# A projection tile loaded one unit earlier, and empty steps ahead of its matmuls, in a two-layer decoder trunk

## The chip, the cores and the metric

The kernel runs on one core of a Trainium2 chip. The metric is the device time of one execution in microseconds; the kernel before took 2547.33 us in the median of three runs (2542.2 to 2547.57). The engines are named as in the profile: PE (TensorE, matmuls; PEld are its weight loads), DVE (VectorE), ACT (ScalarE), POOL (GpSimd) and SP (SyncE, which issues most transfers).

## The reference

A residual stream `x` of 1024 tokens by 1024 passes two layers. Layer 0 mixes with native sparse attention (compressed, selected and windowed branches, 16 heads in 4 groups), layer 1 with a sliding window of 128 and a sink per head. Each mixer ends with an output projection, `o.reshape(B, S, 1024) @ w_out`, then `x = x + (1 + g1) * rms_norm(y, norm_g)`, and a squared-ReLU MLP with hidden size 4096 follows:

```python
y = nsa_mixer(h, ...)            # layer 0;  swa_sink_mixer in layer 1
x = x + (1 + g1)[:, None, :] * rms_norm(y, norm_g[i, 1])
h = modulate(rms_norm(x, norm_g[i, 2]), sh2, sc2)
y = squared_relu_mlp(h, mlp_w_up[i], mlp_w_down[i])
x = x + (1 + g2)[:, None, :] * rms_norm(y, norm_g[i, 3])
```

## The kernel before

**Precision.** A product of float32 matrices is made of three matmuls (`mm3`, L572 to L574): each operand is split in a rounded high part and a low part (the rest), and high x high, low x high and high x low are added up in PSUM.

**Attention.** Both attentions are software pipelines of 32 units (`pipeline`, L940). In layer 0 a unit is a token tile `i` of 128 queries and a head group `j`, in the order j = 0 with i = 0 to 7, then j = 1 and so on, so units 24 to 31 are j = 3. In layer 1 the four groups of one token tile follow each other. A unit has *head* steps (scores on the PE, masking with a running minimum on DVE, L884, exponentials on ACT, L888, scaling on POOL, L1028 or L1626) and *main* steps: a turn (`pv_steps`, L890) transposes four probability blocks on the PE (L903) and splits them into a high part (ACT, L909) and a low part (DVE, L910), and three turns later the products with V follow (L925). The head steps of later units are let out at a rate: the summed cost of all heads over the summed weight of all main entries. Between a unit's turns, `spread` deals out the entries that `more(n)` gives for the unit.

**The end of a unit.** In layer 0 the output of a unit is copied (ACT, L1121) and stored to the DRAM tile `od[i]` by SP (L1122). In layer 1 it stays on the chip: `o_out` copies it (ACT, L934 and L936) and adds both halves on POOL (L938) into `o32[i]`.

**Output projection.** `out_steps(t, ...)` returns `first` and eight matmul steps. `first` gets the tile by `load`, casts it to its high part (L1179, DVE), subtracts for the low part (L1180, DVE) and loads the rows of x (L1183, SP). In layer 0 `load` brings the tile from DRAM in four transfers on SP (L1737) and adds two halves on DVE (L1738). A matmul step is two terms of `mm3`, six matmuls; 48 make a tile of 128 x 1024. Behind them the tile is squared (ACT, L513), multiplied by the gate row (DVE, L514), added to x (L522), stored (L1196), normalised and turned for the MLP.

The projection weights (eight `load` steps, each a 512 KB transfer at L547, a cast on ACT at L565 and a subtraction at L566, on POOL in layer 0 and on DVE in layer 1) come in during attention: in layer 0 as entries of units 26 to 31, in layer 1 two each in units 4 to 7.

**Order.** In layer 0 all projection work follows attention: `outs[0][0]` (the `first` of tile 0) stands after the last unit, then each tile's steps with the next tile's `first` ahead of them. In layer 1 the projection is dealt into later units: after unit 6, 10, 14 and so on, `out(i)` appends `first`, NO empty steps and the eight matmul steps to `extra`, of which the following four units take a share each; the last tile stands behind the last unit. Empty steps count as entries, for the rate and for chains that wait some number of steps (`later`, `TURN`). All large buffers come from one pool of 40. The order of instructions on each engine is laid out in the build by the scheduler of `TileContext` (`schedule_with_timeline_sim=True`), from the program's order and the dependences.

Of the kernel before, what the change touches and what calls it, by code (L numbers as in the profile page):

```python
# [45 lines left out]
W0 = 4  # L46
ON = 2
WP = 1
NO = 1
ML = 0  # L50
RAMP1 = 12
HOLD = 80
# [41 lines left out]
class Trunk:  # L94
# [1549 lines left out]
    def run(self):  # L1644
        nc, a = self.nc, self.a
        tok = lambda t: slice(t * P, (t + 1) * P)
        self.cols, self.gates = {}, {}
        self.mark("setup")
        self.setup()
        xin, xout = a["x"][0], self.out[0]  # L1650
        self.mark("start")
        xr = {}
        def load_x(ts):
            xs = [self.slot(name="x") for t in ts]
            for t, x in zip(ts, xs):
                nc.sync.dma_start(x, xin[tok(t)])
            return xs

        def norm_x(ts, xs):
            for stages in zip(*(self.norm_stages(x, xr, t) for t, x in zip(ts, xs))):  # L1660
                for f in stages:
                    f()

        half = self.ada_first()
        (load0, half0), (load1, half1) = half(0), half(1)
        xs = load_x(range(4))
        rows = self.load_columns()
        w_in = a["nsa_w_in"][0]
        raws = []
        for f in load0:  # L1670
            f()
        for k in (0, 2):
            raws.insert(0, self.raw_weight(self.slot, w_in, [k, k + 1], D, 512))
        self.setup_columns(*rows)
        norm_x(range(4), xs)
        hT = [[], []]
        parts = self.nsa_project(hT, w_in)
        loads, steps = parts[0]
        pre = self.pre_pairs([xr[t] for t in range(4)], self.cols[0, 0], hT[0])
        first = lambda k: [steps[4 * t + k + z] for z in range(2) for t in range(4)]  # L1680
        for k in range(PA):
            pre[k][0]()
        for f in half0:
            f()
        for f in load1:
            f()
        for k in (4, 6):
            raws.insert(0, self.raw_weight(self.slot, w_in, [k, k + 1], D, 512))
        self.raws = raws
        for f in loads[:2]:  # L1690
            f()
        xs = load_x(range(4, NT))
        pre = [g if k < PA else lambda f=f, g=g: (f(), g()) for k, (f, g) in enumerate(pre)]
        self.mark("nsaproj")
        second = half1[:-1] + loads[2:] + half1[-1:]
        self.later(self.turn_tables, 6)
        self.go(pre[:4] + spread(second[:-1], first(0)) + second[-1:])
        norm_x(range(4, NT), xs)
        self.setup_late()
        self.go(pre[4:6] + spread(pre[6:], first(2)[:4]))  # L1700
        for f in self.pre_steps([xr[t] for t in range(4, NT)], self.cols[0, 0], hT[1]):
            self.later(f, 0)
        self.go(first(2)[4:])
        side = self.ada_gate(0, 0) + self.ada_pre(0, 1)
        self.chunks([([], steps[16:])] + parts[1:-1] + [(parts[-1][0], parts[-1][1][:QN])], side, [], S0)
        self.flush()

        src = [xin[tok(t)] for t in range(NT)]
        for l in range(2):
            w_out = a["nsa_w_out" if l == 0 else "swa_w_out"][0]  # L1710
            self.mark("att")
            x1 = [self.tc.dram_tile([P, D], F32, name=f"x1_{l}_{t}") for t in range(NT)]
            xr = {}
            o32 = {}
            grow = {}

            def gate(l=l, grow=grow):
                if not grow:
                    grow[0] = self.gate_row(self.gates[l, 0])
                return grow[0]  # L1720

            take, up = self.up_setup(a["mlp_w_up"][l], lambda l=l: self.cols[l, 1])

            def done(t, x, take=take, xr=xr, l=l):
                def turn():
                    self.chain([lambda: None] * (2 + DL if t == NT - 1 else TURN[l]) + take(t, xr))
                self.chain(self.norm_stages(x, xr, t) + [turn])

            if l == 0:
                loads = self.out_weights(w_out, nc.gpsimd if WP & (l + 1) else None)  # L1730

                def load(t):
                    o = [self.slot("o32", F32, [P, KT, P]) for _ in range(2)]
                    for h in range(2):
                        src = self.od[t][64 * h:64 * h + 64].rearrange("d j (k z) t -> z d (j k) t", z=2)
                        for z in range(2):
                            nc.sync.dma_start(o[h][64 * z:64 * z + 64], src[z])  # L1737
                    nc.vector.tensor_tensor(o[0], o[0], o[1], op=ALU.add)  # L1738
                    return o[0]

                def more(n):
                    return {26: loads[0:1], 27: loads[1:2], 28: loads[2:3], 29: loads[3:5], 30: loads[5:6], 31: loads[6:]}.get(n, [])

                self.nsa_attention(more, parts[-1][1][QN:])
                outs = [self.out_steps(t, lambda t=t: load(t), src[t], gate, x1[t], done) for t in range(NT)]
                self.mark("wout")
                outs[0][0]()
                for t in range(NT):
                    steps = outs[t][1]
                    if t + 1 < NT:  # L1750
                        steps = [outs[t + 1][0]] + steps
                    else:
                        steps = spread(up[-1], steps)
                    self.go(steps)
            else:
                extra, loads = list(parts[-1][1][4 * QT:]), self.out_weights(w_out, nc.gpsimd if WP & (l + 1) else None)

                def out(i):
                    f, steps = self.out_steps(i, lambda: o32.pop(i), src[i], gate, x1[i], done)
                    extra.extend([f] + [lambda: None] * NO + steps)  # L1760

                def more(n):
                    k = -(-len(extra) // ((ON - n) % 4 + 1)) if n > ON else len(extra) // (4 + ON - n)
                    part = extra[:k]
                    del extra[:k]
                    if n >= W0:
                        part = spread(loads[:2], part)
                        del loads[:2]
                    if n % 4 == ON and n > ON:
                        out(n // 4 - 1)  # L1770
                    return part

                self.pipeline([self.swa_unit(i, gg, o32) for i in range(NT) for gg in range(4)], more, LEAD2, RAMP, 0, RS2, LAG2)
                out(NT - 1)
                self.go(spread(up[-1], extra))
            self.mark("mlp")
            xd = [self.tc.dram_tile([P, D], F32, name=f"x2_{t}") for t in range(NT)] if l == 0 else \
                [xout[tok(t)] for t in range(NT)]
            hT2 = [[], []]
            xr2 = {}  # L1780
            g2 = []

            def post(t, y, l=l):
                if not g2:
                    g2.append(self.gate_row(self.gates[l, 1]))
                x = self.slot(name="x")
                nc.sync.dma_start(x, x1[t])
                half, stages = self.gated(lambda h: y[:, h * 512:(h + 1) * 512], lambda: x, lambda: g2[0],
                                          nc.gpsimd if t < (PT if l else PT0) else nc.vector)

                def end():
                    nc.sync.dma_start(xd[t], x)
                    if l == 0:
                        self.finish_tile(t, x, xr2, self.cols[1, 0], hT2)
                half(0)
                half(1)
                self.later(lambda: self.chain(stages + [end]), 1)

            if l == 0:
                parts = self.swa_project(hT2, a["swa_w_in"][0])  # L1800
            side = self.ada_gate(0, 1, True) + self.ada_pre(1, 0, None, True) if l == 0 else self.ada_gate(1, 1, True)
            self.mlp(up, a["mlp_w_down"][l], side, self.ada_gate(1, 0) + self.ada_pre(1, 1) if l == 0 else [], post,
                     parts[0][0] if l == 0 else [])
            if l == 0:
                self.mark("swaproj")
                self.chunks(parts[:-1] + [(parts[-1][0], parts[-1][1][:4 * QT])])
                src = xd
            self.flush()
# [28 lines left out]
```

## Time and profile before

| | |
|---|---|
| median of three runs | 2547.33 us |
| profiled execution | 2548.21 us |
| its span in the profile | 2546.4 us |
| mean granted clock of the PE | 0.977 |
| attention of layer 0, ends with the last L925 | at about 789.8 us |
| projection of layer 0 | 796.17 to about 896 us |
| attention and projection of layer 1 | about 1665 to 1903 us |

Times in a timeline are microseconds from the start of the span. A number in brackets at the end of a line is the idle time of that engine just before it, and after the arrow stands what ended it. Consecutive instructions of one kind are merged in one line, with their count.

### The profile page before, as it was taken

To read this page: it belongs to the slowest core of one execution; us is meant where nothing else is said; L and a number is where in the kernel's file an instruction comes from. 1 tells how busy PE (TensorE), PEld (TensorE's weight loads), DVE (VectorE), ACT (ScalarE), POOL (GpSimd) and SP (SyncE) were. 2 spreads that over 40 slices of the span, in tenths; PEclk is the share of its full clock that TensorE was granted. 3 is DMA by queue.
4 is the path that set the end of the run, shared out by engine and by line. 5 is a ranking of instruction groups with operands and counts; after the bars stand their busy time and mean duration, and the time that the engine had idled before them with its cause. 6 is when DMAs were issued, how large, how long until landed. Compare 5 with 4: busy or idle time off the path is not lost.

```text
span 2546.4 us, 36695 instructions
## 1 busy us (share of the span) xinstructions
PE 2399.9 (94%) x11974; PEld 1991.6 (78%) x11974; DVE 1924.9 (76%) x3723; ACT 1403.2 (55%) x2959; POOL 1325.5 (52%) x1308
## 2 busy tenths in 40 slices
PE   6989999999998988999999999978999899999997
PEld 4779788888887766777778887867877688888886
DVE  7866479999895477877899768667767766787756
ACT  4632268888983463444435445367876355545433
POOL 4320566564672146555764722577744654594533
PEclk8999999999999999999999999998999999999999
DMA  7367723131226635556888754444323545597654
GB/s 279 100 224 229 237 88 96 39 92 42 84 71 149 141 116 189 201 191 201 321 324 324 236 189 163 138 128 125 75 76 128 186 168 183 192 318 240 230 183 173
DMA packets 239288, 437.15 MB, mean 172 GB/s; under 512 B 19236, under 2 KB 122872, under 8 KB 239096
## 3 DMA queue, kind: packets, MB, share of 16 engines
q1 hardware_dynamic: 210296, 405.44, 47.3%
q0 software_dynamic: 28800, 29.36, 4.8%
q8 instruction: 94, 1.54, 0.2%
q14 instruction: 98, 0.80, 0.1%
HBM read 320.42 MB, written 114.31 MB: 171 GB/s over the span
## 4 chain that ended last, share of the span: by engine, by line
PE 40%; DVE 6%; POOL 3%; issue 2%; DMA 2%; ACT 2%; SPq 0%; POOLq 0%; DVEq 0%; ACTq 0%
PE b L574 13%; PE b L572 13%; PE b L573 12%; POOL sx L1415 1%; DVE ada L323 1%; PE b L880 1%; DMA w<-in_mlp_w_up_dram 1%; DVE hl L1251 1%; PE o L925 1%; DVE p L884 1%; PE b L903 1%; DVE wt L1340 1%; DMA adaw<-in_ada_w_dram 0%; POOL qv L637 0%; POOL wr L1473 0%
## 5 line engine op out<-in xcount | busy, mean ns | idle before, releaser
L572 PE MATMUL b<-hh,wt 128*128 128x512 f32 x896 | 355.0, 396 | 17.0 <-ACT wt L1339 16.9
L574 PE MATMUL b<-hh,wt 128*128 128x512 f32 x896 | 350.9, 395 | 11.9 <-DVE wt L1340 11.6
L573 PE MATMUL b<-st,st 128*128 128x512 f32 x896 | 350.3, 391 | 4.9 <-DVE st L1489 4.9
L573 PE MATMUL b<-hl,wt 128*128 128x512 f32 x896 | 352.1, 393 | 0.0
L574 PE MATMUL b<-st,st 128*128 128x512 f32 x896 | 349.0, 390 | 0.0
L572 PE MATMUL b<-st,st 128*128 128x512 f32 x896 | 330.7, 390 | 1.6 <-DVE u L1370 1.6
L888 ACT ACTIVATE p<-p,nm 128x256 f32<-128x256 f32 (+7 forms) x384 | 250.7, 657 | 56.5 <-DVE nm L884 55.3
L1028 POOL TENSOR_SCALAR p<-p,rl,nsam 128x640 f32<-128x640 f32 (+7 forms) x256 | 199.5, 791 | 139.5 <-DVE rl L1026 93.1
L910 DVE TENSOR_TENSOR pT<-b,pT 128x512 fp32r<-128x512 f32 (+1 forms) x334 | 215.0, 657 | 19.5 <-ACT pT L909 19.1
L1488 ACT ACTIVATE st<-wr 128x1024 fp32r<-128x1024 f32 (+1 forms) x128 | 122.6, 958 | 193.2 <-POOL wr L1474 87.4
L1489 DVE TENSOR_TENSOR st<-wr,st 128x1024 fp32r<-128x1024 f32 (+1 forms) x128 | 188.3, 1471 | 53.6 <-ACT st L1488 30.1
L1489 DVE TENSOR_TENSOR st<-sr,st 128x1024 fp32r<-128x1024 f32 (+1 forms) x128 | 200.4, 1566 | 33.0 <-ACT st L1488 30.8
L572 PEld LDWEIGHTS b<-hh,wt 128*128 128x128 f32 x896 | 170.1, 190 | 59.3 <-ACT wt L1339 25.4
L574 PEld LDWEIGHTS b<-hh,wt 128*128 128x128 f32 x896 | 169.9, 190 | 55.7 <-DVE wt L1340 20.5
L909 ACT ACTIVATE pT<-b 128x512 fp32r<-128x512 f32 (+1 forms) x334 | 186.3, 579 | 43.2 <-PE b L903 41.8
L573 PEld LDWEIGHTS b<-st,st 128*128 128x128 f32 x896 | 168.5, 188 | 42.4 <-DVE st L1489 7.8
L903 PE MATMUL b<-ident,p 128*128 128x128 f32 x1296 | 193.5, 273 | 5.7 <-DVE nm L884 4.1
L1340 DVE TENSOR_TENSOR wt<-ws,wt 128x512 fp32r<-128x512 f32 x128 | 139.5, 1101 | 77.4 <-ACT wt L1339 76.8
L572 PEld LDWEIGHTS b<-st,st 128*128 128x128 f32 x896 | 168.6, 188 | 37.2 <-DVE u L1370 2.4
L573 PEld LDWEIGHTS b<-hl,wt 128*128 128x128 f32 x896 | 170.1, 190 | 34.6
L574 PEld LDWEIGHTS b<-st,st 128*128 128x128 f32 x896 | 168.6, 188 | 34.9
L925 PE MATMUL o<-pT,kv 128*128 128x512 f32 x484 | 193.1, 437 | 1.8 <-DVE pT L910 1.4
(277 smaller groups left out, 6060.3 us busy)
## 6 DMA issues: line engine op xcount, KB each, us to landing
adaw<-in_ada_w_dram SPq DMA_DIRECT2D x96, 512.0 KB, 4.9
sr<-s SPq DMA_DIRECT2D x96, 512.0 KB, 4.7
wr<-in_mlp_w_down_dram SPq DMA_DIRECT2D x96, 512.0 KB, 5.9
w<-in_mlp_w_up_dram SPq DMA_DIRECT2D x76, 512.0 KB, 4.8
s<-sx SPq DMA_DIRECT2D x64, 512.0 KB, 4.0
x<-x SPq DMA_DIRECT2D x48, 512.0 KB, 3.8
s<-u SPq DMA_DIRECT2D x64, 256.0 KB, 2.3
we<-in_mlp_w_down_dram SPq DMA_DIRECT2D x64, 256.0 KB, 3.9
```

The source lines that it names most:

```text
L572: mm(out, s[0], m[0], start=first, stop=False)
L573: mm(out, s[0], m[1], start=False, stop=False)
L574: mm(out, s[1], m[0], start=False, stop=last)
L888: self.nc.scalar.activation(p, p, AF.Exp, scale=-1.0, bias=nm, accum_out=l)
L903: nc.tensor.transpose(pt[:, g * P:(g + 1) * P], p[:, cols], self.ident)
L909: nc.scalar.activation(x[:, 0, 0:w], pt[:, 0:w], AF.Copy)
L910: nc.vector.tensor_tensor(x[:, 1, 0:w], pt[:, 0:w], x[:, 0, 0:w].bitcast(F32), op=ALU.subtract)
L925: nc.tensor.matmul(out, s, m[:, z], start=n == 0 and z == 0, stop=n == len(tiles) - 1 and z == 1)
L1028: nc.gpsimd.tensor_scalar(ps[g], ps[g], rl[:, g:g + 1], gate[:, g, b:b + 1], op0=ALU.mult, op1=ALU.mult)
L1340: nc.vector.tensor_tensor(lo, r, hi.bitcast(F32), op=ALU.subtract)
L1488: nc.scalar.activation(hi, r, AF.Copy)
L1489: nc.vector.tensor_tensor(lo, r, hi.bitcast(F32), op=ALU.subtract)
```

## The change

The constant NO goes from 1 to 4. In layer 0, the list of `outs` is built ahead of attention, and the `first` of tile 0 becomes an entry of unit 31, between its two weight steps.

```diff
-NO = 1
+NO = 4
...
                 def more(n):
-                    return {26: loads[0:1], 27: loads[1:2], 28: loads[2:3], 29: loads[3:5], 30: loads[5:6], 31: loads[6:]}.get(n, [])
-
+                    return {26: loads[0:1], 27: loads[1:2], 28: loads[2:3], 29: loads[3:5], 30: loads[5:6],
+                            31: loads[6:7] + [outs[0][0]] + loads[7:]}.get(n, [])
+
+                outs = [self.out_steps(t, lambda t=t: load(t), src[t], gate, x1[t], done) for t in range(NT)]
                 self.nsa_attention(more, parts[-1][1][QN:])
-                outs = [self.out_steps(t, lambda t=t: load(t), src[t], gate, x1[t], done) for t in range(NT)]
                 self.mark("wout")
-                outs[0][0]()
                 for t in range(NT):
```

## Rows read from the trace of the kernel before

**Rows 1.** The page, part 1: busy time, share of the span, instructions.

```profile
PE 2399.9 (94%) x11974; PEld 1991.6 (78%) x11974; DVE 1924.9 (76%) x3723; ACT 1403.2 (55%) x2959; POOL 1325.5 (52%) x1308
```

**Rows 2.** Timeline of the PE at the seam of layer 0: start, length, line.

```profile
785.37 1.26 PE L925 MATMUL o<-pT,kv 128*128 128x512 f32 x4
786.86 2.89 PE L925 MATMUL o<-pT,kv 128*128 128x512 f32 x9 [0.22 <-DVE pT L910]
796.17 0.77 PE L572 MATMUL b<-wh,oh 128*128 128x512 f32 x1 [6.43 <-DVE oh L1179]
...
799.73 0.42 PE L572 MATMUL b<-wh,oh 128*128 128x512 f32 x1
799.99 0.39 PE L573 MATMUL b<-wl,oh 128*128 128x512 f32 x1
800.22 0.40 PE L574 MATMUL b<-wh,ol 128*128 128x512 f32 x1
```

**Rows 3.** Windows: length, busy of PE, PEld, DVE, ACT, POOL, clock, DMA, GB/s.

```profile
794.00:798.00 4.00, 1.83 (x4) 1.49 (x5) 3.15 (x3) 0.00 (x0) 0.00 (x0) 0.50 1.14 280
```

**Rows 4.** Timeline of SP, 760 to 790: transfers as they are issued.

```profile
765.05 0.37 SPq L547 DMA_DIRECT2D w<-in_mlp_w_up_dram  x1
779.21 0.34 SPq L1122 DMA_DIRECT2D o<-otmp  x1
782.84 0.37 SPq L547 DMA_DIRECT2D w<-in_mlp_w_up_dram  x1
783.31 2.86 SPq L1737 DMA_DIRECT2D o<-o  x4
```

**Rows 5.** Timeline of DVE, 775 to 806.

```profile
777.76 2.91 DVE L910 TENSOR_TENSOR pT<-b,pT 128x512 fp32r<-128x512 f32 x5 [1.23 <-ACT pT L909]
783.70 1.89 DVE L910 TENSOR_TENSOR pT<-b,pT 128x512 fp32r<-128x512 f32 x3 [3.04 <-ACT pT L909]
786.11 3.08 DVE L910 TENSOR_TENSOR pT<-b,pT 128x512 fp32r<-128x512 f32 x5 [0.52 <-ACT pT L909]
794.00 1.23 DVE L1738 TENSOR_TENSOR o<-o,o 128x1024 f32<-128x1024 f32 x1 [4.81 <-DMA o<-o]
795.33 0.69 DVE L1179 CAST oh<-o 128x1024 fp32r<-128x1024 f32 x1
796.06 1.23 DVE L1180 TENSOR_TENSOR ol<-o,oh 128x1024 fp32r<-128x1024 f32 x1
...
804.69 0.69 DVE L1179 CAST oh<-o 128x1024 fp32r<-128x1024 f32 x1
```

**Rows 6.** L1737's landings; waits of L1738; L1737's issues from 780 to 796.

```profile
DMA to landing us min/median/max: 4.2/6.6/10.1
...
  DMA o<-o: 32.1, 7
...
o<-o SPq DMA_DIRECT2D x8, 256.0 KB, 8.1
```

**Rows 7.** Timelines of ACT and DVE, 840 to 852.

```profile
844.15 0.20 ACT L513 ACTIVATION_READ_ACCUMULATOR junk<-b 128x1 f32 x1
...
849.06 1.22 DVE L1738 TENSOR_TENSOR o<-o,o 128x1024 f32<-128x1024 f32 x1 [7.15 <-DMA o<-o]
850.20 0.68 DVE L514 TENSOR_TENSOR yg<-b,gbc 128x512 f32<-128x512 f32 x1
```

**Rows 8.** Timeline of the PE in layer 1, 1720 to 1730.

```profile
1722.93 0.80 PE L572 MATMUL b<-wh,oh 128*128 128x512 f32 x1 [3.86 <-DVE oh L1179]
1726.37 0.79 PE L574 MATMUL b<-wh,ol 128*128 128x512 f32 x1 [2.22 <-DVE ol L1180]
```

**Rows 9.** Windows in layer 1, columns as in rows 3.

```profile
1715.00:1720.00 5.00, 2.97 (x8) 1.83 (x8) 5.00 (x13) 4.44 (x12) 5.00 (x7) 0.50 0.70 239
1720.00:1725.00 5.00, 1.22 (x2) 0.50 (x2) 5.00 (x14) 4.94 (x16) 4.98 (x7) 0.50 0.86 236
1725.00:1730.00 5.00, 3.63 (x9) 2.85 (x10) 3.90 (x6) 0.56 (x2) 4.79 (x5) 0.50 1.09 260
```

**Rows 10.** Waits of the PE, 1730 to 1910: total us, times, longest.

```profile
PE b L572 <- DVE oh L1179: 2.5, 1, 2.5
PE b L880 <- DVE nm L884: 1.6, 2, 1.3
```

## The prediction

> **What bounds the kernel now.** I read the busy shares first. The PE works 94% of the span, and no other engine gets past 76% [rows 1]. So a microsecond is gained where the PE stands still or runs at the half clock, and hardly anywhere else. I then went to the two seams that the diff touches, with the timelines of PE, DVE and SP side by side, and with the windows for the clock.
>
> At the seam of layer 0, the last attention matmuls end at 789.75, and the first projection matmul starts at 796.17 after 6.43 us of idle, released by the cast of L1179 [rows 2]. The clock falls meanwhile (0.50, that is 1.2 GHz, from 794 to 798 [rows 3]), and the first eight projection matmuls need 3.56 us, where a later one starts 0.23 us after the one before [rows 2]: 3.56 - 8 x 0.23 = 1.7 us lost. The reader should see why the cast is late. SP issues the four loads of L1737 from 783.31 to 786.17, behind a weight load at 782.84, though it did nothing between 765.42 and 779.21 [rows 4]. Then the add of L1738 waits 4.81 us for them until 794.00, and add, cast and subtraction end at 797.29, 3.3 us later [rows 5].
>
> In layer 1, the first projection tile stops the PE for 3.86 us (its cast) and again for 2.22 us (its low half) [rows 8]. Around it DVE, ACT and POOL are all but full and the clock is at 0.50 [rows 9]. The last tile waits another 2.5 us [rows 10].
>
> **Part 1: the first tile goes into unit 31.** Its step issues four loads and the load of x on SP, and add, cast and subtraction on DVE. Three entries spread over 17 steps stand at steps 0, 6 and 12 (two stood at 0 and 9). So the tile comes after the sixth turn, whose DVE copy ends at 780.67 [rows 5], and the last weight step moves from 9 to 12. That weight is needed only late in tile 0, so I cost its move at nothing.
>
> What it costs on DVE: the 3.3 us now stand ahead of eight copies of L910 (three from 783.70, five from 786.11, 4.97 us together). DVE has a hole of 3.04 us there [rows 5]. If the loads have landed by 780.67, the copies slip by 0.3 us. If not, DVE waits at the add, and the copies wait behind it. That an instruction behind it does wait is seen later in this stage: the multiplication of L514 had its input at 844.35, but ran at 850.20, after the add had waited 7.15 us and run [rows 7].
>
> So the term hangs on the landing. The loads take 4.2 us at least, 6.6 in the median, and 8.1 for those issued at this seam [rows 6]. Three cases, each with 13 attention matmuls [rows 2] and 48 projection matmuls to follow (61 x 0.23 = 14.0 us), against tile 0's end today at 799.73 + 40 x 0.23 = 808.9:
> - Early: SP runs ahead of the other engines and issues before 779.21. Nothing is late; the matmuls run on from 785.37, and tile 0 ends at 785.4 + 14.0 + 0.3 = 799.7. Gain 9.2 us.
> - Middle: SP issues right behind the copy-out of 779.21, four times 0.71 us from 779.55 [rows 4], the last at 781.7. It lands at 785.9; DVE is through at 789.2; one copy of 0.62 us frees the PE at 789.8, and tile 0 ends at 803.8. Gain 5.1 us, or 3.4 if the idle of some 4 us brings the half clock again.
> - Late: 8.1 us of landing, so 789.8, 793.1, 793.7, 807.7. Gain 1.2 us, or a loss of 0.5 with the clock. If moreover the tile's matmuls don't fill the gaps between the copies (793.1 + 5.0 + 0.5 + 11.0 + 1.7 = 811.3), a loss of 2.4.
>
> I take the middle with half of the clock's loss, 4.3 us, because the queue is otherwise idle there and the nearest row for an idle queue is the 4.2. The ends for the range are +9.2 and -2.4. The Trainium skill, page "DMA: Bandwidth & Descriptors", section "Anatomy of one DMA", gives a transfer about 2.0 us plus its bytes at 436 GB/s, fitted on another issuing engine; an estimate by it is 2.6 us for 256 KB. By that page the gain of the middle case would be 6.7 instead of 5.1 us; the row's 4.2 decides here.
>
> What is late next: tile 1 has its cast done at 805.38 [rows 5], and the middle case wants it at 803.8. Since tile 0's megabyte has left that stretch, I expect tile 1's loads earlier too and cost this at nothing; without that it is 1.6 us. The later loads wait for DMA 32.1 us in seven adds [rows 6], but SP issues them behind stores that themselves follow the earlier tiles, so they move with tile 0.
>
> One entry more in unit 31 also lowers the rate at which `pipeline` lets score steps out, by one part in some 330 over the whole attention of layer 0. Score steps run 42 cost units ahead, so this is nothing, or a few tenths either way.
>
> **Part 2: four empty steps in layer 1.** The split stays at the same step; the eight matmul steps behind it move. Over the four units they were dealt 1, 3, 2, 2 and are now 0, 2, 3, 3. No instruction is added. The entries of all units grow from some 146 to 165, so score steps come out more slowly per entry (0.77 to 0.68 cost units), and the chains that count steps run out a little sooner against the work; I cost both at nothing, as buffers and leads stay.
> - Tile 0: of 3.86 + 2.22 = 6.1 us of idle, I take half, 3.0 us. The PE gets other work to do first, but from 1715 to 1725 DVE (5.00 of 5), ACT and POOL are full [rows 9], so there may be little to feed it. Ends: 6.1 and 0.
> - The clock: 3.63 us of PE work from 1725 to 1730 at 0.50 [rows 9] would take half at full clock. I take 0.9; ends 1.8 and 0.
> - The last tile: one more step (six matmuls, 1.4 us) of tile 6 is left to stand in its 2.5 us. I take 1.0; ends 2.5 and 0.
> - New gaps: the first unit behind each split has one projection step fewer. If the PE idled each time, it would cost 7 x 1.4 = 9.8 us. The other waits of the PE from 1730 to 1910 are short, the longest sum 1.6 us [rows 10], so other work does come forward, and I take nothing; for the range I allow a third, 3 us.
>
> Sum for layer 1: 3.0 + 0.9 + 1.0 = 4.9 us (ends 10.4 and -3).
>
> **Sum.** 4.3 + 4.9 = 9.2 us. The profiled execution took 2548.21 us (span 2546.4 and 1.8 around it), 0.88 above the median of the three runs, 2547.33. So 2539.0 for it, and 2538.1 for a median.
>
> **The rivals.**
> - *DVE stands at the add (slower).* The loads still go out behind the weight load at 782.84, land at 794.0 as now, and now eight copies stand behind the add: 797.3 + 5.0 + 0.5, then 48 matmuls of 0.23, 813.8, and with the half clock 815.5 instead of 808.9. That is 4.9 to 6.6 us lost, and with nothing won in layer 1 about 2553. It decides if the loads land after some 791, 1.2 us beyond the late case. For it: the wait of 4.81 and the blocked L514 [rows 5, 7]. Against it: SP is idle until 779.21 [rows 4], and what the loads read was stored seven units earlier. Beside it, the Trainium skill, "Perfetto Trace Analysis", section "Tensor Engine Instruction", says that ACT, DVE and GPSIMD execute strictly first in, first out; by that rule the copies can't pass the add, and rows 7 agree.
> - *Layer 1 gives nothing.* The three full engines set the pace there, and the PE waits for their copies instead of the split. Then 2547.33 - 4.3 = 2543.0. For it: [rows 9]; against it: ACT drops to 0.56 of 5 from 1725 on, while the PE works through the late tile.
> - *The change doesn't do what it says.* The instruction order is laid out by the scheduler of the build and not by the program alone; if it leaves loads and matmuls where they are, both parts give nothing: 2547.3. That it does move work is seen where a weight load of the MLP stands ahead of these loads [rows 4].
>
> **How the numbers follow.** No change is anything within 0.2%, 5.1 us (2542.2 to 2552.4); a measurement of this kernel can tell no less. The forecast has 0.68, with times from 2529 to 2542. Layer 1 giving nothing has 0.15, no effect at all 0.08 and the blocked DVE 0.09, half of whose size falls short of 5.1 us if layer 1 gives anything. Faster 0.69, same 0.24, slower 0.07. The low end takes both parts near their upper ends (9.2 + 8.5), the high end holds the second and third rival; what is left out is the blocked DVE and a little below 2529.
>
> **What would show it.** Right: the idle before the first L572 of the seam is below 3 us, tile 0 ends by 804, the four L1737 stand before 782.84 on SP, and in layer 1 the waits of 3.86 and 2.22 us are gone while PE work from 1715 to 1725 rises above 4.2 us. Wrong: a wait of DVE on DMA ahead of L1738 above 6 us with L910 right behind it, or a PE that waits at 1715 to 1730 for L884 or L910 as long as it did for L1179.

## The result, and the profile after

The changed kernel takes 2574.29 us (median of 4 runs, 2573.07 to 2576.64) where the kernel before took 2546.05 beside it: a ratio of 1.0112, 95% interval 1.010 to 1.0125, or 28.5 us slower (25.5 to 31.8). Forecast were 2538.1 us; the slowest case that the forecast range was to hold, no effect at all, was 2547.3. The profiled span is 2571.9 us, 25.5 more than before.

The page's part 1 of the kernel after shows the same matmuls and 1.3 us less PE work than [rows 1], so what was added is idle time of the PE:

```profile
PE 2398.6 (93%) x11974; PEld 1995.3 (78%) x11974; DVE 1931.6 (75%) x3723; ACT 1407.8 (55%) x2959; POOL 1334.7 (52%) x1308
```

**Layer 0, the seam.** First SP's timeline of the kernel after:

```profile
778.30 0.37 SPq L547 DMA_DIRECT2D w<-in_mlp_w_up_dram  x1
778.86 1.23 SPq L1737 DMA_DIRECT2D o<-o  x2
780.19 0.62 SPq L1122 DMA_DIRECT2D o<-otmp  x1
780.90 1.24 SPq L1737 DMA_DIRECT2D o<-o  x2
782.24 0.70 SPq L1183 DMA_DIRECT2D x<-in_x_dram  x1
783.03 4.85 SPq L1737 DMA_DIRECT2D o<-o  x4
...
804.27 0.33 SPq L1122 DMA_DIRECT2D o<-otmp  x1
804.68 2.56 SPq L1737 DMA_DIRECT2D o<-o  x4
...
818.35 0.33 SPq L1196 DMA_DIRECT2D x<-x  x1
818.79 2.93 SPq L1737 DMA_DIRECT2D o<-o  x4
...
833.94 0.32 SPq L1196 DMA_DIRECT2D x<-x  x1
834.31 2.84 SPq L1737 DMA_DIRECT2D o<-o  x4
```

The first tile's loads go out from 778.86 instead of 783.31 [rows 4]. But tile 1's four follow at 783.03, while they land. DVE and then the PE, same kernel:

```profile
777.93 2.92 DVE L910 TENSOR_TENSOR pT<-b,pT 128x512 fp32r<-128x512 f32 x5 [0.31 <-ACT pT L909]
789.64 1.58 DVE L1738 TENSOR_TENSOR o<-o,o 128x1024 f32<-128x1024 f32 x1 [8.79 <-DMA o<-o]
791.25 0.69 DVE L1179 CAST oh<-o 128x1024 fp32r<-128x1024 f32 x1
791.98 1.23 DVE L1180 TENSOR_TENSOR ol<-o,oh 128x1024 fp32r<-128x1024 f32 x1
793.12 4.87 DVE L910 TENSOR_TENSOR pT<-b,pT 128x512 fp32r<-128x512 f32 x8
```

```profile
793.86 1.22 PE L925 MATMUL o<-pT,kv 128*128 128x512 f32 x2 [9.04 <-DVE pT L910]
...
796.59 0.63 PE L572 MATMUL b<-wh,oh 128*128 128x512 f32 x1
```

The add waits 8.79 us where it waited 4.81 [rows 5], with all eight copies behind it (the sign of being wrong that the prediction names), and the PE waits 9.04 us for the first of them where it waited 6.43 for the cast [rows 2]. The first projection matmul comes at 796.59 (before: 796.17), the second tile's at 811.15 (before: 808.87).

**Layer 0, the later tiles.** A window from the first matmul of tile 4 to the end of tile 7 (columns as in [rows 3]), before and then after:

```profile
843.40:896.35 52.95, 50.77 (x233) 40.79 (x231) 24.17 (x40) 21.21 (x56) 10.30 (x12) 0.97 0.51 123
```

```profile
845.68:903.95 58.27, 50.81 (x233) 39.27 (x232) 26.79 (x44) 25.20 (x68) 10.85 (x13) 1.00 0.55 136
```

Another 5.3 us are lost in the last four tiles, all of it idle PE. With the 2.3 us of the seam, layer 0's projection ends 7.6 us later.

**Layer 1.** A window over the whole attention and projection stage, from the first score matmul to the end of tile 7, before and then after:

```profile
1662.70:1903.00 240.30, 211.75 (x1124) 176.32 (x1123) 173.49 (x507) 185.16 (x526) 161.91 (x247) 0.93 0.36 97
```

```profile
1669.90:1927.70 257.80, 212.01 (x1124) 179.07 (x1123) 173.43 (x505) 186.98 (x526) 167.21 (x247) 0.92 0.33 89
```

The stage is 17.5 us longer with the same PE work; idle rises from 28.6 to 45.8 us. The waits of the PE from 1660 to 1925 (us, times, longest), before and then after:

```profile
PE b L880 <- DMA qs<-qd: 9.7, 3, 7.5
PE b L572 <- DVE oh L1179: 6.4, 2, 3.9
```

```profile
PE b L880 <- DMA qs<-qd: 34.6, 6, 11.3
PE b L880 <- ACT pT L909: 3.3, 1, 3.3
PE o L925 <- ACT pT L909: 1.8, 1, 1.8
PE b L572 <- DVE oh L1179: 1.5, 1, 1.5
```

The waits for the split shrank as intended. In their place score matmuls (L880) wait for q, the queries of a token tile, which POOL loads from DRAM (L875). The longest such wait, in the timelines of POOL and then of the PE after:

```profile
1817.91 1.49 POOL L938 TENSOR_TENSOR o<-otmp,olo 64x256 f32<-64x256 f32 x2 [4.66 <-ACT olo L936]
1819.48 0.57 POOL L451 TENSOR_TENSOR r<-ms,mhalf 128x1 f32<-128x1 f32 x1
...
1824.76 0.55 POOL L451 TENSOR_TENSOR r<-ms,mhalf 128x1 f32<-128x1 f32 x1 [0.43 <-DVE ms L450]
1825.27 1.89 POOL L875 DMA_DIRECT2D qs<-qd  x2
```

```profile
1829.16 2.05 PE L880 MATMUL b<-K,qs 128*128 128x256 f32 x8 [11.30 <-DMA qs<-qd]
1831.01 0.63 PE L572 MATMUL b<-wh,oh 128*128 128x512 f32 x1
```

The load of q stands in POOL's queue behind the merges of finished units (L938) and the norm of a finished tile (L451). The PE stands for 11.30 us at the score that needs it, with tile 3's matmuls behind that score.

### The profile page after: what moved, and what is told of

Read it like the earlier page. It is cut to its first block, busy times and chain, and to the rows that moved or that the text cites. A ratio compares the mean times of both kernels' runs of the same rounds, so it can differ in the third digit from the quotient of the medians.

```text
span 2571.9 us, 36696 instructions
## 1 busy us (share of the span) xinstructions
PE 2398.6 (93%) x11974; PEld 1995.3 (78%) x11974; DVE 1931.6 (75%) x3723; ACT 1407.8 (55%) x2959; POOL 1334.7 (52%) x1308
## 5 line engine op out<-in xcount | busy, mean ns | idle before, releaser
L909 ACT ACTIVATE pT<-b 128x512 fp32r<-128x512 f32 (+1 forms) x334 | 186.5, 581 | 52.4 <-PE b L903 50.3
L572 PEld LDWEIGHTS b<-hh,wt 128*128 128x128 f32 x896 | 170.5, 190 | 57.6 <-ACT wt L1339 23.4
L925 PE MATMUL o<-pT,kv 128*128 128x512 f32 x484 | 193.8, 439 | 10.7 <-DVE pT L910 10.4
L903 PE MATMUL b<-ident,p 128*128 128x128 f32 x1296 | 196.2, 275 | 2.3 <-DVE pT L910 1.3
```

Of the source, the lines that this page charges most:

```text
L572: mm(out, s[0], m[0], start=first, stop=False)
L903: nc.tensor.transpose(pt[:, g * P:(g + 1) * P], p[:, cols], self.ident)
L909: nc.scalar.activation(x[:, 0, 0:w], pt[:, 0:w], AF.Copy)
L925: nc.tensor.matmul(out, s, m[:, z], start=n == 0 and z == 0, stop=n == len(tiles) - 1 and z == 1)
```

## Experiments

Differences in us below are a run's ratio times its comparison's median (2544 to 2547 us); "stage" is layer 1's window as above, cut at each run's own ends. The stage less its idle time is the busy time of the PE. The matmuls are the same in every row, so more busy time means, for the most part, that more of them ran at the half clock. Five runs whose layer 1 is that of the kernel before (e1, e6, e7, e9, e10) have stages of 238.2 to 239.0 us, 28.4 to 29.4 of them idle; a difference of 2 us in the last column says nothing.

| run | median us | ratio (95%) | layer 1: stage, PE idle |
|---|---|---|---|
| kernel before | 2546.1 | 1 | 240.3, 28.6 |
| changed kernel | 2574.3 | 1.0112 (1.010 to 1.0125) | 257.8, 45.8 |
| e1, layer 0's part | 2552.3 | 1.0026 (1.0017 to 1.0035) | |
| e2, layer 1's part | 2566.4 | 1.0077 (1.0062 to 1.0092) | 258.1, 44.4 |
| e3, e2 with the score rate kept | 2557.8 | 1.0045 (1.0030 to 1.0059) | 250.1, 32.7 |
| e4, e2 with lead 22 | 2550.8 | 1.0017 (1.0007 to 1.0026) | 242.4, 34.3 |
| e5, e2 with q three ahead | 2554.0 | 1.0034 (1.0023 to 1.0044) | 246.8, 31.8 |
| e12, e3 and e5 together | 2557.5 | 1.0049 (1.0034 to 1.0063) | 248.3, 33.6 |
| e13, e2 with q on SP | 2543.2 | 0.9995 (0.9985 to 1.0005) | 234.9, 27.5 |
| e14, before with q three ahead | 2550.9 | 1.0017 (1.0007 to 1.0028) | 244.5, 32.5 |
| e8, before with lead 22 | 2559.5 | 1.0049 (1.0034 to 1.0064) | 252.8, 37.3 |
| e11, two empty steps | 2546.3 | 1.0001 (0.9990 to 1.0012) | 237.4, 26.6 |
| e15, three empty steps | 2554.5 | 1.0042 (1.0027 to 1.0057) | 244.6, 32.0 |
| e6, early loads | 2541.8 | 0.9981 (0.9971 to 0.9991) | |
| e7, step first in unit 31 | 2546.2 | 1.0001 (0.9992 to 1.0011) | |
| e9, e1 with stores on ACT | 2538.4 | 0.9977 (0.9966 to 0.9987) | |
| e10, e6 with stores on ACT | 2533.6 | 0.9956 (0.9941 to 0.9971) | |
| e16, e10 with q on SP | 2524.9 | 0.9923 (0.9908 to 0.9938) | 234.2, 22.0 |
| e17, e16 with four empty steps | 2533.0 | 0.9954 (0.9940 to 0.9969) | 238.6, 30.2 |
| e18, e16 with two empty steps | 2522.4 | 0.9916 (0.9895 to 0.9937) | 232.6, 23.9 |

### The two parts alone

e1, against the changed kernel:

```diff
-NO = 4
+NO = 1
```

> Only the first tile of layer 0 moves into unit 31; layer 1 keeps one empty step. Theory (two separate losses; in layer 0 DVE stands at the add with eight copies behind it and the late tiles lose more): tile 0 to the end of the projection in layer 0 as in the changed kernel, 7 to 8 us later, so about 2554 us, and the first tiles of layer 1 late by that alone. Rival A (the disturbed layer 0 also causes the loss in layer 1, by other buffers and another order): 2565 us or more. Rival B (layer 1's empty steps are the whole loss, and layer 0 gets its time back in the MLP): within 3 us of 2546.

e2, against the kernel before:

```diff
-NO = 1
+NO = 4
```

> Only the four empty steps in layer 1; layer 0 as in the kernel before. Theory: the waits of the PE for loads of q stay (27 us in five waits in the changed kernel), and the time is about 2546 + 17 = 2563 us. Rival A (the loss comes over from layer 0): within 3 us of 2546, or below by the 4.9 us that I had forecast. The first idle of 6.1 us at the projection's start should shrink to some 2 in both.

e1 loses 6.6 us (4.3 to 8.9), e2 19.6 (15.8 to 23.4); together 26.2, against 28.5 of the whole. The losses are separate: e2's stage in layer 1 is as long as the changed kernel's (258.1 and 257.8) with layer 0 untouched. Rivals A and B fall.

### Layer 0: what costs the time

e7, against e1: the step as the first entry of the unit.

```diff
-                            31: loads[6:7] + [outs[0][0]] + loads[7:]}.get(n, [])
+                            31: [outs[0][0]] + loads[6:]}.get(n, [])
```

> One empty step in layer 1. In layer 0 the whole step of the first tile (loads, add, cast, subtraction) stands as the first entry of unit 31 instead of the second, ahead of twelve copies on DVE instead of eight. Theory of the add: the loads go out earlier by some 3 us and the add's wait falls from 8.2 to about 5 us, but more copies stand behind it; 2548 to 2553 us. Rival (any place in unit 31 is as good): the same as the run of layer 0 alone, 2552 us within 1.

One entry earlier was enough to let SP issue into its empty stretch. SP and DVE of e7:

```profile
766.77 2.58 SPq L1737 DMA_DIRECT2D o<-o  x4
```

```profile
774.59 1.91 DVE L1738 TENSOR_TENSOR o<-o,o 128x1024 f32<-128x1024 f32 x1 [0.53 <-DMA o<-o]
```

The wait is 0.53 us, not the 5 that I expected, and both of my forecasts (2548 to 2553, and 2552 within 1) were missed. The first projection matmul comes at 789.84, 6.3 us before that of the kernel before. Some 2 us of this are no gain of the seam: e7 reaches layer 0's first transpose (L903) at 312.6 already, the kernel before at 314.6. Yet the projection ends at 896.16, where it ended at 896.35, and the time is that of the kernel before. So the seam is not what sets the end of this stage. The pace behind it is: e7's last four tiles start 13.0, 14.3 and 14.2 us apart, although a tile occupies the PE for 11.8.

e6 keeps add, cast and subtraction behind the attention in the program and moves the four loads alone:

```diff
-                def load(t):
-                    o = [self.slot("o32", F32, [P, KT, P]) for _ in range(2)]
+                got = {}
+
+                def fetch(t):
+                    got[t] = o = [self.slot("o32", F32, [P, KT, P]) for _ in range(2)]
...
-                    return {26: ..., 31: loads[6:]}.get(n, [])
+                    return {26: ..., 31: [lambda: fetch(0)] + loads[6:]}.get(n, [])
```

(`load` then takes what is in `got`.)

> One empty step in layer 1. In layer 0 only the four loads of the first tile go ahead, to the start of unit 31; add, cast and subtraction stay in the program behind the attention, and the load of x with them. Theory (DVE stands at the add because SP issues the loads late): with the loads ahead of the copy-out of 779.2 they land by 788 at the latest, DVE hardly waits, tile 0 starts at 792 or earlier instead of 796.2, and the time is 2540 to 2545 us. Rival (the pace of layer 0 is set by the loads of the later tiles behind the stores, so an earlier first tile is given back): the first tile earlier by 3 us or more, the projection's end unmoved, 2545 to 2549 us.

The first matmul comes at 788.60, and 4.8 us are won (2.3 to 7.4). Part of the seam's gain reaches the end here. In both runs the loads had landed in time or nearly so, but in e6 tile 0's update L522 runs at 806.39, ahead of tile 2's add at 809.56; in e7 it runs at 809.31, behind that add. What this update sets off comes next.

What sets the later pace is on SP. In the rows of the changed kernel above, the last copy-out of the attention (L1122) goes out at 804.27 with tile 2's loads right behind it; then every tile's loads stand right behind the store (L1196) of the tile three before it. The same queue in the kernel before:

```profile
798.41 4.61 SPq L1737 DMA_DIRECT2D o<-o  x4
812.79 0.33 SPq L1196 DMA_DIRECT2D x<-x  x1
...
813.72 3.09 SPq L1737 DMA_DIRECT2D o<-o  x4
...
826.88 0.33 SPq L1196 DMA_DIRECT2D x<-x  x1
827.30 2.79 SPq L1737 DMA_DIRECT2D o<-o  x4
```

There the copy-out is through at 790.40, tile 2's loads go at 798.41, and the stores come at 812.79 and 826.88 instead of 818.35 and 833.94. Each store waits on SP for the update L522, which stands on DVE behind the add of a tile still being loaded, as DVE of e1 shows (L514 feeds L522):

```profile
810.00 1.22 DVE L1738 TENSOR_TENSOR o<-o,o 128x1024 f32<-128x1024 f32 x1 [5.41 <-DMA o<-o]
811.14 0.68 DVE L514 TENSOR_TENSOR yg<-b,gbc 128x512 f32<-128x512 f32 x1
...
814.29 1.28 DVE L522 SCALAR_TENSOR_TENSOR x<-yg,r,x 128x1024 f32<-128x1024 f32 x1 [0.47 <-POOL r L451]
```

That is a ring: load, add, update and store follow each other, and the store lets out the next load. e9 breaks it at the store, against e1:

```diff
-                    nc.sync.dma_start(xdst, u["x"])
+                    (nc.scalar if self.early else nc.sync).dma_start(xdst, u["x"])
```

(`self.early` is true in layer 0.)

> The run of layer 0 alone (first tile's whole step second in unit 31, one empty step in layer 1), with one thing changed: the eight stores of the finished tiles in layer 0 are issued on ACT's queue, which waits for the same data anyway, instead of SP's, where the loads of the tile three further on stand behind them. Theory (the loss of part 1 is made not at the seam but in tiles 4 to 7, whose loads wait behind stores that have become later): tiles 4 to 7 come every 11.8 us again instead of 13.2 to 16.6, and the 5.3 us are gone or turned into a gain: 2538 to 2547 us. Rival (DVE's wait at the seam itself costs the 5 us): 2551 us or more.

e9's window from tile 4 to the end:

```profile
843.34:891.69 48.35, 48.35 (x234) 40.23 (x233) 26.51 (x43) 25.20 (x62) 10.29 (x12) 1.00 0.34 97
```

The PE is never idle. These tiles come 11.8 us apart, and the whole is 5.9 us faster than the kernel before, with DVE still standing at the seam's add (8.89 us). The ring is the cause of the later loss; the rival falls. The gain over the kernel before is the ring's too, and not part 1's: the second tile starts at 808.80 here and at 808.87 there, and the kernel before already runs into the ring (tiles 6 and 7 take it 13.0 and 16.3 us, e9 11.8 and 12.9). That kernel with its stores on ACT was not run. e10 joins e6 and e9:

> The run with only the loads of the first tile ahead (2541.8 us), and the eight stores of layer 0 on ACT's queue as well. Theory of the loads behind the stores: tile 0 starts at 788.6 as there, every tile takes 11.8 us, and the projection ends near 885 instead of 891.7; 2533 to 2538 us. Rival (the later loads wait for buffers and not for the queue): 2540 us or more, with the SP waits put down to another engine.

11.2 us are won (7.4 to 15.0), and from tile 2 on the tiles come 11.8 us apart. The first starts at 791.75, 3.2 us later than in e6, and the end is 888.07 instead of the expected 885: this run came to the seam 3.2 us later as a whole (its first loads go out at 769.63, those of e6 at 766.45).

### Layer 1: why the loads of q are late

e3, against e2: an empty step weighs nothing in `rate`.

```diff
-            mains.append(spread([(MW, f) for f in more(n)],
+            mains.append(spread([(0.0 if f is None else MW, f or (lambda: None)) for f in more(n)],
...
-                    extra.extend([f] + [lambda: None] * NO + steps)
+                    extra.extend([f] + [None] * NO + steps)
...
```

> Four empty steps in layer 1 as in the run before it, but an empty step weighs nothing in the count by which score steps are let out, so that their rate per entry is that of no empty step at all (slightly above the kernel before). Theory of the rate (fewer score steps ahead, so loads of q come later): most of the 17 us come back, 2542 to 2549 us, and the waits for q sink below 5 us. Rival (the moved matmuls and the buffers that they hold longer delay the loads of q): still 2555 us or more, with waits for q above 15 us.

e4 (against e2) and e8 (against the kernel before) have the same edit. LEAD2 is the number of cost units by which the score steps of layer 1 run ahead; the head of a unit costs 3.5.

```diff
-LEAD2 = 18
+LEAD2 = 22
```

> Four empty steps in layer 1 with the diluted rate, and the lead of the score steps raised from 18 to 22 cost units, a little over one unit of attention. Theory of the rate: the raised lead makes up for it, 2542 to 2550 us. Rival (buffers are short, all but one or two of the 40 are taken): more score steps ahead hold more buffers, and the time stays at 2560 us or rises.

> The kernel before with one thing changed: the lead of layer 1's score steps is 22 cost units instead of 18. If a larger lead is good by itself, the same 15 us that it gave back with four empty steps show here too, or a part: below 2541 us. If 18 was enough at the old rate, nothing: 2547 within 4. If buffers are short, slower than 2551.

The kept rate gives back 8 of 19.6 us: by the time (2557.8 us) that is the rival's case, by the waits for q (13.6 us from 1660 to 1925, e2 34.4) it lies between both. What is left is mostly not idle time: the PE is idle for 32.7 us and busy for 217.4, more than in any other row. Nor is the rate quite the old one: when the 12th unit's scores start, 40 transposes of earlier units are done in e3 and 44 in the kernel before.

The larger lead gives back 15 us, a little less than expected, and not by the waits for q alone, which stay long:

```profile
PE b L880 <- DMA qs<-qd: 29.3, 9, 7.5
```

That is 5 us less than in e2. The other waits of the PE sink nearly as much, and its busy time from 213.7 to 208.1. And with one empty step the same lead costs 12.5 us, which I had as the third possibility only. So lead is no good by itself: 18 cost units fit the old rate, 22 the diluted one. The rate decides part of the loss, and too much lead costs time as too little does.

e11 and e15, against the kernel before, take two and three empty steps:

```diff
-NO = 1
+NO = 2
```

> The kernel before with two empty steps in layer 1 instead of one. Theory of the rate: the score rate sinks by a quarter as much as with four (one of the three steps added makes a third), so a third of the 19.5 us, 2551 to 2555 us. Rival (the order falls one way or the other with any small change, and the count of empty steps says little): anything from 2540 to 2565, above all faster than before.

```diff
-NO = 1
+NO = 3
```

> Three empty steps in layer 1; one cost nothing more than two (2546 each) and four 19.5 us. Theory (a load of q misses its score only once the lead is smaller by some amount): the waits for q begin here, 2550 to 2562 us. Rival (chance of the order): 2546 or less, without new waits for q.

Two steps cost nothing, three 10.7 us, four 19.6. I had expected with e11 that the loss follows the rate step by step, and missed: the rate sinks with the first step added, the loss begins when loads of q come too late. After the stage's first wait for q (7.5 and 7.6 us) e15 waits 13.0 us more for q, 5.9 the longest; e11 waits 1.7.

e5, against e2, puts the loads out earlier (the argument replaces the constant `QA` in layer 1 alone); e14 is the same against the kernel before, e12 is e3 and e5 together:

```diff
-                while q < len(units) and q <= n + QA:
+                while q < len(units) and q <= n + qa:
...
-                self.pipeline([...], more, LEAD2, RAMP, 0, RS2, LAG2)
+                self.pipeline([...], more, LEAD2, RAMP, 0, RS2, LAG2, 3)
```

> Four empty steps in layer 1 with the diluted rate and the lead of 18, but the loads of q are put out three units ahead of their scores instead of one. Theory (what costs the time is that loads of q come late, behind the norm chain on POOL, and the PE stands in order at the score): the PE's waits for q in the projection's stage go below 5 us and the time comes back to 2546 to 2553 us. Rival (the smaller lead of the scores as a whole costs it: with q there, the PE stands at transposes and copies of the same late units): 2560 us or more, with other waits in the place of those for q.

> A control: the kernel before with loads of q three units ahead, one empty step. If what this costs by itself (its first wait for q was 10.8 us where it is 7.5 in the kernel before) explains what was left in the runs with four empty steps: 2550 to 2556 us. If it costs nothing by itself, 2544 to 2548 us, and the moved matmuls keep the rest.

> Four empty steps in layer 1 that weigh nothing in the score rate, and the loads of q three units ahead: both remedies. Theory (late loads of q cost the time, and the smaller lead is one of their causes): the waits for q are gone and the time is 2540 to 2550 us. Rival (the moved matmuls cost 11 us by themselves, through PSUM banks and copies): as with the rate alone, 2555 us or more.

Waits of the PE in e5 from 1660 to 1925:

```profile
PE b L880 <- DMA qs<-qd: 10.7, 1, 10.7
PE o L925 <- DVE nm L884: 4.8, 3, 2.2
```

The waits for q in the projection's stage are gone (one is left, at the stage's start, where more loads stand at once), and 11 of the 19.6 us with them; the time, 8.7 us over the kernel before, lies a little above what I expected. The control, e14, has the same first wait of 10.7 us and costs 4.3 us by itself. That leaves about 4 us, if the two add up. In the traces the stages differ by 2.3 us, and not by idle time. The stage in e5 and then in e14:

```profile
1661.00:1907.80 246.80, 214.99 (x1124) 179.15 (x1123) 170.98 (x505) 184.87 (x526) 170.52 (x247) 0.92 0.34 93
```

```profile
1662.20:1906.70 244.50, 211.99 (x1124) 176.35 (x1123) 173.39 (x507) 185.41 (x526) 164.14 (x247) 0.93 0.34 95
```

The PE is idle for 31.8 and 32.5 us, but busy for 215.0 and 212.0: with four empty steps more of the same matmuls ran at the half clock (granted 0.92 and 0.93). Both remedies together (e12) give no more than one, and by its time that is the rival's case. No wait for q is left there but the first (10.8 us); the PE waits for DVE and ACT instead (L884 6.6 us, L909 4.4) and is busy for 214.7. So late loads of q are not all that the moved matmuls can cost.

e13 tests the queue. It takes the loads off POOL, against e2; the same tiles are loaded, and the `bitcast` makes both sides of the load float32:

```diff
-                self.nc.gpsimd.dma_start(self.qs[:, z], src[z][:, :, c:c + P])
+                self.nc.sync.dma_start(self.qs[:, z].bitcast(F32), src[z][:, :, c:c + P])
```

> Four empty steps in layer 1 with the diluted rate and the lead of 18, q one unit ahead as before, but layer 1's loads of q are issued on SP's queue instead of POOL's. Theory (the loads are late because they stand on POOL behind the merges of finished units and the norm chain): the PE's waits for q after 1700 fall from 27 us to below 10, and the time is 2546 to 2556 us. Rival (they are late because buffers come free late, or because they are put out late in the program): the waits and the 2566 us stay.

The time is back, and more than I expected: 2543.2 us, 1.3 less than the kernel before (within its interval of no change), and the stage:

```profile
1662.10:1897.00 234.90, 207.39 (x1124) 174.74 (x1123) 170.45 (x505) 184.96 (x526) 146.59 (x220) 0.96 0.31 97
```

PE idle falls from e2's 44.4 to 27.5 us, and the granted clock is 0.96 instead of 0.91. POOL has 20 us less to do. A load itself is no faster on SP: from issue to landing it takes 3.7 us in the median, and 3.6 in e2 (from 1690 to 1880). The waits for q were expected below 10 us after 1700 and are 15.0: the loads still stand in an in-order queue, now that of SP.

e16 is e10 with this edit; e17 and e18 are e16 with NO = 4 and NO = 2:

> The fastest run so far (first tile's loads early, layer 0's stores on ACT's queue, one empty step; 2533.6 us) with layer 1's loads of q on SP. If the queue of POOL delays loads of q in the kernel before as well: up to 2 us of its later waits for q go, and POOL is free for 24 x 0.8 us more; 2527 to 2533 us. If not, 2533 to 2537 us.

> The fastest version (2524.9 us: layer 0's loads early, its stores on ACT's queue, layer 1's loads of q on SP) with four empty steps in layer 1 instead of one. If what I forecast for part 2 holds once the loads of q are off POOL's queue (the PE's 5.3 and 2.5 us at L1179 go, nothing else comes): 2519 to 2523 us. If the lead is too small on any queue (5.5 and 7.3 us of waits for q were left in the run with four steps on SP's queue): 2526 to 2533 us.

> The same with two empty steps. The wait at L1179 is halved and the lead is hardly smaller: 2521 to 2525 us. If the order falls badly: up to 2533.

e16 takes 2524.9 us, 8.4 less than e10 and below what I expected. So POOL's queue had cost time with one empty step too, and of the 21 us between e2 and e13 some 8 have nothing to do with the three steps added. Like compared with like, four empty steps cost about 8 us on SP's queue (e17 against e16; 3 to 13 by both intervals), where they cost 19.6 on POOL's. Two may win 2 (the intervals overlap). With four the waits for q are back. Those of the PE from 1650 to 1925 in e16 and then in e17:

```profile
PE b L880 <- DMA qs<-qd: 4.6, 1, 4.6
```

```profile
PE b L880 <- DMA qs<-qd: 22.2, 5, 9.4
```

Where the longest comes from shows e17 on SP and on the PE:

```profile
1784.44 0.33 SPq L1196 DMA_DIRECT2D x<-x  x1
1784.86 15.17 SPq L875 DMA_DIRECT2D qs<-qd  x4
```

```profile
1789.35 2.04 PE L880 MATMUL b<-K,qs 128*128 128x256 f32 x8 [9.45 <-DMA qs<-qd]
```

Here the loads of q stand behind a store that waits for its update, and the PE stands 9.45 us. The two fastest versions, e16 and e18, are faster than both kernels of this case. Stores of layer 1 on ACT's queue, which should take this wait away too, were not tried.

## Why the prediction was wrong

**The seam of layer 0.** Issues came as forecast for the middle case: the last of the four at about 781.5, forecast 781.7. The step that failed is the landing, "the nearest row for an idle queue is the 4.2". The queue was not left idle: in the changed kernel these four took 5.4 to 8.1 us, with a weight load just ahead of them and x and tile 1's four loads behind, and the add began at 789.64. Nor does 4.2 hold for four at once on an idle queue: in e7, with nothing issued by SP for 7 us behind them, they took 4.6 to 5.7. The late case had 789.8 from the row of this very seam (8.1), and its lowest end 811.3 for tile 0 and a loss of 2.4 us; measured are 811.15 and 2.3. I had both rows and took the kinder one.

**The later loads, "so they move with tile 0".** I cost them at nothing, and that was the larger error of part 1: 5.3 us. I had read that SP issues them behind stores that follow earlier tiles, and took it for a harmless chain. (The 32.1 us in seven adds that I read there hold tile 0's own 4.81; the later adds wait 27.3 us in six.) It is a ring with DVE and SP in it, and it runs slower (14.3 us a tile) than the PE (11.8). The start it gets decides how early the PE runs into it, and e7 shows that a start some 4 us earlier (6.3 by the clock of the trace) is given back. A gain at the head of a stage counts only if the stage's last tile moves.

**The slower rival of part 1.** It had the mechanism, a DVE that stands at the add with eight copies behind it, and 4.9 to 6.6 us; measured are 6.6 (e1). That the size agrees is luck: at the seam only 2.3 us were lost, with a landing before 791, and two thirds of the loss were made later, in the ring that it does not have. The rule it cites from the Trainium skill, "Perfetto Trace Analysis", section "Tensor Engine Instruction" (ACT, DVE and GPSIMD strictly in order), agrees with the trace: no copy passed the add that waited 8.79 us, and POOL's load of q did not pass the L451 that waits for DVE.

**Layer 1, the tile waits.** These were right, the sizes on the low side: the first tile's 3.86 and 2.22 us became 1.55 and 0.61, a gain of 3.9 us where 3.0 was taken, and the last tile's 2.5 is gone, where 1.0 was taken.

**Layer 1, what was cost at nothing.** The step that failed is "score steps come out more slowly per entry (0.77 to 0.68 cost units) ...; I cost both at nothing, as buffers and leads stay". In place of nothing, the waits for q rose from 9.7 to 34.6 us and the stage grew by 17.5. The lead stays as a number but counts against entries, and empty entries dilute it: when the 12th unit's scores start, 48 transposes of earlier units are done where 44 were. Half a unit less is little for the scores, but a load of q is put out one unit ahead and then stands on POOL behind work of other units. POOL's queue is shown to carry the larger part: four empty steps cost 19.6 us with it and about 8 without (e16, e17), where loads of q wait on SP's queue instead. Whether it was the place behind L938 and L451 or the 20 us that issuing the loads takes of POOL's time, no run separates; the rows of the longest wait show the place. The rate is shown to be one cause of being late (8 us in e3), and e4 and e8 that the lead has to fit it. The 3 us allowed for new gaps were a guess about the projection's own steps; the gaps came at the scores.

**The half clock.** I took 0.9 us of gain. The stage's granted clock went from 0.93 to 0.92, so nothing was gained. After the new wait of 11.30 us the granted clock is 0.50 again (from 1829 to 1831), and the projection matmuls from 1831.01 to 1833.1 take 0.63 us each, later ones 0.39. Across the runs this term is larger than I allowed for: the stage's busy PE time goes from 207.4 us (e13) to 217.4 (e3).

What stays open: why a lead of 22 costs 12.5 us at the old rate. The trace of e8 has longer waits for q (21.0 us, before 9.7), one of 8.1 us for DVE's L1617 and 3.7 us more of busy PE, but no run takes them apart. Nor is it known how much of the 19.6 us is a misfit of constants that had been set for each other: e3, e5, e8, e12 and e14, which change the rate, the lead or the place of q's loads in the program, all lose 4 to 13 us against the kernel before.

## What to carry to other kernels

An in-order queue makes every instruction wait for what the one ahead of it waits for, so before moving a step, list for each queue what stands behind it that somebody needs soon: a load on a queue that also carries stores or merges is only as early as those. A gain at the head of a stage is kept only if the slowest ring of that stage (here load, add, update, store on one queue) is faster than the engine that bounds it; look at the spacing of the last tiles first. And empty steps are not free where other work is paced by the count of steps.

## What the runs showed of the hardware beside that

- A DVE instruction can take several times its usual length while POOL works: in e6 the cast of L1179 took 2.86 us at 785.59 instead of 0.69, while a subtraction (L566) ran on POOL from 785.48 to 787.90. The cast ended 0.55 us after it; e10, e16 and e18 show the same pair, with casts of 2.81 to 2.84 us. The Trainium skill, "SBUF — State Buffer", section "SBUF: two separate sides", says that a DVE instruction in a two-port mode shares a port pair with GpSimd, and that the one that starts first holds it for its whole instruction while the other is blocked. These rows agree, if the cast ran in such a mode, which no row tells.
- The store costs ACT next to nothing: 0.33 us each in e9, and ACT waits for the same update in its next instruction anyway (36.0 us in eight waits).
- A load of q kept POOL 0.74 to 1.15 us when POOL issued it. Without them POOL's busy time in layer 1 falls from 167.0 (e2) to 146.6 us (e13).
